# Query tiles 0 to 3 made in the gates' ring, and the attention's remaining projections spread over its units

## The chip, the cores and the metric

The kernel runs on one core of one Trainium2 chip. The core has a matrix engine (TensorE, PE in the profile; its weight loads are PEld), a vector engine (DVE), a scalar engine (ACT), GpSimd (POOL) and a queue engine (SyncE, SP) that here only issues DMAs. Every engine carries out its instructions in the order in which they stand; engines wait for each other on semaphores. The metric is the device time of one execution in microseconds, lower is better, as the median of the runs.

## The reference

One layer of a decoder trunk, in fp32, on 2048 tokens of width 1024:

```python
u = x * (1.0 + scale) + shift                       # from silu(c) @ w_ada + b_ada
q, k, v, a_gate, p_in, p_gate, m_a, m_p = split(u @ w_in)
a = sliding_window_sink_attention(q, k, v, sinks, bias, mask) * silu(a_gate)   # 16 heads of 64, 2 k/v heads, window 128
a = a @ w_attn_proj
p = group_linear(multiscale_causal_pool(p_in))      # windows 2, 4, 8, 16
p = (p * pool_scale) * silu(p_gate)
p = p @ w_pool_proj
y = ((sigmoid(m_a) * a + sigmoid(m_p) * p) @ w_out) * (1.0 + gate)
out = layer_norm(2 ** 0.25 * x + y)
```

## The kernel before

**Halves and stages.** The tokens are worked in two halves of 1024 (s = 0, 1), each in two parts of 512 columns (t = 0, 1). For each half there is a *ring* (functions `first_phase` and `second_phase`) and an *attention* (`attention`); then a stage that multiplies out both halves. In the trace the first ring lasts to about 417 us, the first attention to about 683, the second ring to 1018 and the second attention to about 1283.

**Products of three.** Each fp32 product is made of three matmuls on operands that are split in a high and a low part (`mm3`). The split of a weight is one ACT copy and one subtraction on DVE or POOL. A *k-step* is one block of 128 rows of the inner dimension: three matmuls of 128x512.

**The ring** makes two weight tiles of 128 outputs (a `Quad`, from here on a *pair*) for both parts of a half at once, by seven products of half size instead of eight: each product has 4 k-steps, 12 matmuls. So a pair takes 84 matmuls where four plain projections (two tiles by two parts, 8 k-steps each) take 96. Its weights need three splits of 1024 columns and one of 512, and four sums on POOL. A pair's four results come in PSUM banks or in SBUF (`p5`) and are handed to a `consume` function. Pairs are worked in groups of two; near the end there is a group with one pair, and a last group of two. A pair's weights lie in tiles W (two buffers) and A. Functions in `hooks` run other work at given ticks of the ring, counted from its start or, with a negative group number, in its last groups.

**What the ring makes.** The four gates for all tokens (16 pairs, results to DRAM in `gates_d`) and k with v (one pair). After its last group, `first_q` makes query tile 0 for both parts by plain projection, 48 matmuls.

**The attention** goes through 64 *units* n: head pair j = n // 8, part t, block b of 128 queries. In unit n, PE makes the scores of n (`lg<-kk,qs`), the transposes of unit n−2's weights (`pt<-ident,L`), a share of a projection, and the value products of n−2 (`pv<-pth,vv` and `pv<-ptl,vv`). ACT copies one half of the values of n−3 (`o<-pv`), scales rows, makes `pth`, and makes the exponentials (`L<-L,nm`). DVE makes the reciprocal (`sm`), adds the outputs (`o<-pv,o`), reduces the scores (`L<-lg,bt,nsink`), makes `ptl`, and scales rows. The projections are those of the pool input (`mix` tiles 0 to 7, whose weight lies split in DRAM) and of query tiles 1 to 7 (`q`, whose weight is loaded to W and split by one ACT copy and one POOL subtraction). Each tile is made for t = 0 and t = 1, a *slot* of 8 k-steps each. Before, the 30 slots fill units 0 to 59 with 4 k-steps in each unit; then the next stage's first products follow.

**What a finished slot sets off.** A query slot is *taken* (`take_q`: two ACT instructions and two DVE instructions `qs<-mm,qs`, which start when ACT's are done). A mix slot is copied by ACT (`vb<-mm` with two small copies), summed by POOL (`nxt`), reduced by DVE (`nxt<-nxt,mm`, the pool difference) and multiplied by POOL with its gate (`p<-nxt,pg`). The calls stand at the end of a unit, behind the unit's own work on each engine. Bias tiles (`bt<-e_rep`), gates and mix weights are loaded by SP.

Most instructions carry the line of a helper that keeps their program order (L56), so the profile is read by tile names. The functions, with the profile's line numbers:

Of the kernel before, what the change touches and what calls it, by code (L numbers as in the profile page):

```python
# [19 lines left out]
P = 128  # L20
# [39 lines left out]
def kernel(  # L60
# [60 lines left out]
    pin_d = [set_store(f"pin{s}") for s in range(2)]  # L121
    gates_d = {n: dp.tile([2, KT, 2, P, CH], F32, name=f"{n}_d") for n in ("ag", "pg", "ma", "mp")}
    y_d = dp.tile([S // P, P, KT, P], F32, name="y_d")

# [6 lines left out]
    def low(engine, dst, src, hi):  # L131
        engine.tensor_tensor(dst, src, as32(hi), ALU.subtract)  # L132
# [187 lines left out]
    def by_two(t):  # L320
        return t.rearrange("p (a c) -> p a c", a=2)
# [139 lines left out]
    def defer(ticks, f):  # L461
        due.append((now[0] + ticks, len(due), f))
# [269 lines left out]
    def moving_u():  # L732
        return (sets["B11"], sets["B21"]), (sets["T2"], sets["B22"])

    def first_q(ph, turn=None):

        raw, hi, lo = ph.spare(), ph.split(), ph.split()
        nc.sync.dma_start(raw, win[TQ])
        nc.scalar.copy(hi, raw)
        low(nc.vector, lo, raw, hi)  # L740
        accs = []
        for us in moving_u():
            acc, part = projection(us)
            part((hi, lo), 0, KT)
            if turn and not accs:
                turn(1)
            accs.append(acc)
        return accs

    def attention(ph, s, q0, nxt):  # L750
# [8 lines left out]

        def fetch(kind, m):  # L760
            hi, lo = ph.split(), ph.split()
# [107 lines left out]

        slots = []  # L870
        for j in range(KT):
            slots += [("mix", j, 0), ("mix", j, 1)]
            if j + 1 < KT:
                slots += [("q", j + 1, 0), ("q", j + 1, 1)]
# [8 lines left out]
        tiles = {0: fetch(*slots[0][:2])}  # L883
        parts, accs, sums = {}, {}, {}
# [36 lines left out]
        for n in range(N + 5):  # L921
            j, t, b = n // U, n // NB % 2, n % NB
            if n < N:
                lgs[n] = score_mms(j, n % U, b, qs[j, t])
# [71 lines left out]

            w = n // 4 + 1
            if n % 4 == 0 and 2 * w < len(slots):
                tiles[w] = fetch(*slots[2 * w][:2])
            if w in tiles and tiles[w][0] is not None:  # L1000
                raw, hi, lo = tiles[w]
                if n % 4 == 1:
                    act.copy(by_two(hi), raw)
                if n % 4 == 2:
                    low(pool, by_two(lo), raw, by_two(hi))
            if n % U == 2 and j + 1 < KT:
                bts[j + 1] = bias_tile(j + 1)
            for st in range(2):
                if n % U == 6 + 2 * st - (U if st else 0) and (m := j + 1 - st) < KT and ("q", m, st) in accs:
                    qs[m, st] = take_q(accs.pop(("q", m, st)))  # L1010
            for what in puts:
# [12 lines left out]
            for st in range(2):  # L1024
                if n % U == 3 + 2 * st and (j, st) in sums:
                    pgs[j, st] = ld("pg", gates_d["pg"][s, j, st])
                if n % U == ((4, 6 + (j + 1 < KT))[st]) and (j, st) in sums:
                    pl = pool_diff(j, sums.pop((j, st)), accs.pop(("mix", j, st)))
                    finish("p", pin_d[s], j, st, pl, pgs.pop((j, st)))
            for st in range(2):  # L1030
                if n % U == 2 + 2 * st and ("mix", j, st) in accs:
                    sums[j, st] = pool_sums(j, st, accs["mix", j, st])
            for x in [x for x in outs if n == x[0] * U + x[1] * NB + NB + 2]:
# [83 lines left out]
    def modulate(u, k):  # L1117
        dve.tensor_scalar(u, u, mod[:, 8 + k : 9 + k], mod[:, k : k + 1], ALU.mult, ALU.add)

    def gate_quads(s):  # L1120
        kv, turn = kv_quad(s)
        quads = [kv] if s else []
# [3 lines left out]
        last = quads[15:] if s else [kv, quads[15]]  # L1126
        return [quads[i : i + 2] for i in range(0, 14, 2)] + [quads[14:15], last], turn

# [14 lines left out]
    def head(ph):  # L1143
# [92 lines left out]

        groups, turn = gate_quads(0)
        grp = groups[0]
# [72 lines left out]
        ]  # L1311
        return groups, turn, opened, cb, rest

    def first_phase(ph, groups, turn, opened, cb, rest):
        hooks = {}
# [29 lines left out]
    def second_phase(ph, opened, groups, turn):  # L1345
        hooks = {(0, (8, 10)[i]): [lambda i=i: turn(i)] for i in range(2)}
# [29 lines left out]
        for half in range(2):  # L1376
            hooks.setdefault((-1, 3 + half), []).append(lambda half=half: fill_set("T2", half, u1_d["B12"]))
        return ring(ph, groups, opened, hooks, [], lambda tick: first_q(ph), True)

# [13 lines left out]
    def cols2(t, n):  # L1393
        return t[:, n * D : (n + 1) * D]
# [117 lines left out]
```

## Time and profile before

| | before |
|---|---|
| median of 3 runs | 1763.04 us (1761.94 to 1768.7) |
| the profiled execution | 1766.1 us, span 1763.9 us |
| mean clock of PE | 0.991 of full |
| PE, PEld | 97%, 81% of the span |
| DVE, ACT, POOL | 68%, 53%, 45% |
| DMA | 381.3 MB, 216 GB/s |

A row of the instructions in order of time has the start in us, the length in us, the engine, the line, the operation, output <- inputs by the program's names, the shape, how many instructions were merged into the row, and in brackets the idle time of the engine before it with what ended that. The length of a matmul is modelled and overlaps the next one's, so PE's pace is read from the starts.

### The profile page before, as it was taken

Reading aid. Unit: us, or ns where it says so; the run is one execution under the profiler, and the core shown is the slowest. Engines: PE = TensorE matmul, PEld = TensorE weight load, DVE = VectorE, ACT = ScalarE, POOL = GpSimd, SP = SyncE. Lnnn points to the kernel's source line nnn. Section 1 sums busy time; section 2 is a strip of 40 time slices with the busy share of each in tenths; the row PEclk is TensorE's granted clock in tenths of the full one; section 3 lists DMA queues with packets and bytes.
Section 4 is the critical chain, followed back from the end, with each engine's and each line's share of the span. In section 5 each row is a group of like instructions: output and inputs, shape, how many; then the busy total and the mean of one; then the engine's idle time right before and its main releaser. Section 6 shows DMA issues by size and latency. Waiting matters only on the chain. (4 is left out here: it accounts for less than half of the span.)

```text
span 1763.9 us, 24990 instructions
## 1 busy us (share of the span) xinstructions
PE 1702.4 (97%) x8248; PEld 1427.4 (81%) x8248; DVE 1206.9 (68%) x2178; ACT 934.1 (53%) x1973; POOL 794.2 (45%) x618
## 2 busy tenths in 40 slices
PE   6899999999999998999999999999999989999997
PEld 5688888878888887888788888888888867888785
DVE  5977665655777776766655367777867676764777
ACT  4644444545777775544444377777734343423452
POOL 2154444431356567534434125456763562364542
PEclk9999999999999999999999999999999999999998
DMA  9385767844354567787777634544796675789442
GB/s 364 117 289 174 269 208 270 273 145 132 108 174 147 171 217 288 249 288 253 258 264 261 232 96 135 177 159 141 265 349 215 197 256 169 240 302 386 162 143 108
DMA packets 180466, 381.30 MB, mean 216 GB/s; under 512 B 18785, under 2 KB 39281, under 8 KB 180337
## 3 DMA queue, kind: packets, MB, share of 16 engines
q1 hardware_dynamic: 173696, 363.92, 60.5%
q0 software_dynamic: 3552, 11.56, 1.7%
q10 hardware_dynamic: 3088, 4.23, 0.8%
q8 instruction: 65, 1.06, 0.3%
q14 instruction: 65, 0.52, 0.1%
HBM read 244.35 MB, written 138.44 MB: 217 GB/s over the span
## 5 line engine op out<-in xcount | busy, mean ns | idle before, releaser
L56 PE MATMUL mm<-set_B,w_set 128*128 128x512 f32 x3240 | 798.7, 395 | 14.5 <-ACT u L376 6.3
L56 PEld LDWEIGHTS mm<-set_B,w_set 128*128 128x128 f32 x3240 | 603.3, 189 | 142.6 <-DVE w_set L132 10.3
L56 PE MATMUL lg<-set_T,w_set 128*128 128x512 f32 x2088 | 509.1, 394 | 18.4 <-DVE w_set L132 11.0
L56 PEld LDWEIGHTS lg<-set_T,w_set 128*128 128x128 f32 x2088 | 391.4, 189 | 111.0 <-DVE w_set L132 17.9
L132 DVE TENSOR_TENSOR w_set<-W,w_set 128x1024 fp32r<-128x1024 f32 x162 | 227.9, 1407 | 185.8 <-ACT w_set L325 180.8
L325 ACT CAST w_set<-W 128x1024 fp32r<-128x1024 f32 x162 | 169.8, 1049 | 251.6 <-PE mm L56 190.3
L56 PE MATMUL mm<-set_T,w_set 128*128 128x512 f32 x1080 | 265.5, 394 | 0.0
L56 PEld LDWEIGHTS mm<-set_T,w_set 128*128 128x128 f32 x1080 | 200.5, 188 | 41.0
L294 POOL TENSOR_TENSOR W<-W,A 128x512 f32<-128x512 f32 x56 | 82.1, 1466 | 227.6 <-DMA W<-in_win_dram 63.6
L303 POOL TENSOR_TENSOR W<-W 128x512 f32<-128x512 f32 x56 | 80.5, 1438 | 174.5 <-DVE w_set L132 165.2
L56 DVE TENSOR_TENSOR o<-pv,o 64x128 f32<-64x128 f32 x256 | 72.3, 283 | 89.8 <-ACT o L56 86.9
L56 ACT ACTIVATE L<-L,nm 128x257 f32<-128x257 f32 (+1 forms) x256 | 127.1, 498 | 9.3 <-DVE nm L56 3.9
L298 POOL TENSOR_TENSOR W<-W 128x512 f32<-128x512 f32 x56 | 90.5, 1618 | 84.7 <-DVE w_set L132 75.6
L56 DVE CUSTOM_DVE_ANT_0 L<-lg,bt,nsink 128x256 f32<-128x256 f32 (+1 forms) x256 | 111.6, 473 | 5.0 <-PE lg L56 0.8
L299 POOL TENSOR_TENSOR W<-W 128x512 f32<-128x512 f32 x56 | 84.7, 1513 | 37.9 <-DMA W<-in_win_dram 21.9
L56 POOL TENSOR_TENSOR w_set<-W,w_set 128x1024 fp32r<-128x1024 f32 x14 | 33.7, 2404 | 139.6 <-ACT w_set L56 96.9
L56 POOL TENSOR_TENSOR p<-nxt,pg 128x512 f32<-128x512 f32 x32 | 41.7, 1302 | 105.5 <-DVE sm L56 101.8
L56 ACT COPY o<-pv 64x256 f32<-64x256 f32 x128 | 47.3, 370 | 78.0 <-PE pv L56 77.2
L56 DVE TENSOR_TENSOR ptl<-pt,pth 128x512 fp32r<-128x512 f32 (+1 forms) x128 | 85.7, 669 | 1.9 <-ACT pth L56 1.7
L56 PE MATMUL lg<-kk,qs 128*128 128x256 f32 (+1 forms) x512 | 80.5, 279 | 0.0
L56 ACT ACTIVATE L<-L,sm 128x256 f32<-128x256 f32 (+1 forms) x128 | 64.2, 502 | 29.8 <-DVE sm L56 29.8
L56 ACT CAST pth<-pt 128x512 fp32r<-128x512 f32 (+1 forms) x128 | 73.5, 574 | 10.3
(212 smaller groups left out, 2296.3 us busy)
## 6 DMA issues: line engine op xcount, KB each, us to landing
W<-in_win_dram SPq DMA_DIRECT2D x48, 512.0 KB, 5.5
w_set<-wmix_d SPq DMA_DIRECT2D x32, 512.0 KB, 5.4
W<-in_win_dram SPq DMA_DIRECT2D x34, 256.0 KB, 3.7
A<-in_win_dram SPq DMA_DIRECT2D x34, 256.0 KB, 5.1
ag_d<-sig SPq DMA_DIRECT2D x32, 256.0 KB, 3.8
pg_d<-sig SPq DMA_DIRECT2D x32, 256.0 KB, 4.0
ma_d<-sig SPq DMA_DIRECT2D x32, 256.0 KB, 4.0
mp_d<-sig SPq DMA_DIRECT2D x32, 256.0 KB, 4.0
```

Source lines behind the costliest of these rows:

```text
L56: return lambda *args, **kw: self.tc.keep_in_program_order(op(*args, **kw))
L132: engine.tensor_tensor(dst, src, as32(hi), ALU.subtract)
L294: e.tensor_tensor(self.w[:, 1, :], self.w[:, 2, :], self.a22, ALU.add)
L298: e.tensor_tensor(x[:, 1, :], x[:, 1, :], x[:, 0, :], ALU.subtract)
L299: e.tensor_tensor(x[:, 2, :], x[:, 0, :], x[:, 2, :], ALU.subtract)
L303: e.tensor_tensor(x[:, 3, :], x[:, 3, :], x[:, 1, :], ALU.subtract)
L325: a.copy(by_two(hi), raw)
```

## The change

Query tiles 0 to 3 are no longer projected by themselves. They are two more pairs (`q_quad`) at the end of the ring: tiles 2 and 3 in the group of one pair, tiles 0 and 1 in the last group (with k and v in the first half). Tile 0's two results stay in PSUM and are taken at the attention's start; the six results of tiles 1 to 3 go to DRAM (`q_d`) by SP and are loaded again (`raw_q`) two units ahead of their takes, at units 6, 8, 14, 16, 22 and 24. `first_q` is gone. The attention keeps the eight mix tiles and query tiles 4 to 7, 24 slots, in a written order. Their 192 k-steps are spread over units 0 to 59: 6 in unit 0, made ahead of its scores, 4 in units 5, 12, 19, 26, 32, 39, 46, 53 and 59, and 3 in the others. Query tiles are taken in the unit after their last k-step, pool sums are made in that unit too, and pool differences three or four units after the last k-step. The first mix tile is loaded into a W tile instead of two `w_set` tiles.

```diff
-    def first_q(ph, turn=None):
-        ...
+        order = (("mix", 0), ("mix", 1), ("mix", 2), ("mix", 3), ("mix", 4), ("q", 4), ("mix", 5), ("q", 5), ("q", 6), ("mix", 6), ("q", 7), ("mix", 7))
+        slots = [(kind, m, st) for kind, m in order for st in range(2)]
...
+        def upto(n):
+            return (0 if n == 0 else min(n + 1, 61)) * KT * len(slots) // 61
+
+        def unit_of(k):
+            return next(n for n in range(60) if upto(n + 1) > k)
+
+        first = [unit_of(KT * i) for i in range(len(slots))]
+        done = {x: unit_of(KT * i + KT - 1) for i, x in enumerate(slots)}
+
+        def project(n):
+            k = upto(n)
+            while k < upto(n + 1):
+                i = k // KT
+                end = min(KT * (i + 1), upto(n + 1))
+                if k == KT * i:
+                    accs[slots[i]], parts[i] = projection(us[slots[i][2]])
+                parts[i](tiles[i // 2][1:], k - KT * i, end - KT * i)
+                k = end
+
+        room = ph.weights().rearrange("p a c -> p (a c)").bitcast(F32R)
+        tiles = {0: fetch(*order[0], [cols2(room, n) for n in range(2)])}
...
         for n in range(N + 5):
             j, t, b = n // U, n // NB % 2, n % NB
+            if n == 0:
+                project(n)
             if n < N:
                 lgs[n] = score_mms(j, n % U, b, qs[j, t])
...
-            i = n // 2
-            if i < len(slots):
-                kind, m, st = slots[i]
-                if n % 2 == 0:
-                    accs[kind, m, st], parts[i] = projection(us[st])
-                parts[i](tiles[i // 2][1:], 4 * (n % 2), 4 * (n % 2) + 4)
+            if 0 < n < 60:
+                project(n)
...
+            for m in range(1, 4):
+                for st in range(2):
+                    at = 8 * m - 2 + 2 * st
+                    if n == at - 2:
+                        raw_q[m, st] = ld("raw_q", q_d[s][m, st])
+                    if n == at:
+                        qs[m, st] = take_q(raw_q.pop((m, st)))
+            for x in [x for x in done if x[0] == "q" and n == done[x] + 1]:
+                qs[x[1:]] = take_q(accs.pop(x))
...
+                if n == at + 3 + (st == 1 and m + 1 < KT):
+                    pl = pool_diff(m, sums.pop((m, st)), accs.pop(x))
+                    finish("p", pin_d[s], m, st, pl, pgs.pop((m, st)))
...
+    def q_quad(s, m, first):
+        def consume(ph, mi, t, src):
+            k = m + mi
+            if k == 0:
+                first[t] = src
+                return
+            x = src
+            if (mi, t) != (1, 1):
+                x = ph.c("qk")
+                nc.scalar.copy(x, src)
+            defer(2, lambda: sp.dma_start(q_d[s][k, t], x))
+        return Quad((win[TQ + m], win[TQ + m + 1]), consume)
...
+        quads += [q_quad(s, m, q0) for m in (2, 0)]
+        if s == 0:
+            quads.insert(-1, kv)
...
-        return ring(ph, groups, opened, hooks, [], lambda tick: first_q(ph, turn))
+        ring(ph, groups, opened, hooks, [], lambda tick: turn(1))
+        return q0
```

How this stands in the engines' streams is seen at three places. PE in the second attention, before, at units 30 and 31 (scores, transposes, projection, values):

```order
L56 MATMUL lg<-kk,qs 128x256 x4
L56 MATMUL pt<-ident,L 128x128 x4
L56 MATMUL mm<-set_T_235,w_set 128x512 x12
L56 MATMUL pv<-pth,vv 128x256
L56 MATMUL pv<-ptl,vv 128x256
L56 MATMUL pv<-pth,vv 128x256
L56 MATMUL pv<-ptl,vv 128x256
L56 MATMUL lg<-kk,qs 128x256 x4
L56 MATMUL pt<-ident,L 128x128 x4
L56 MATMUL mm<-set_B_576,w_set 128x512 x12
```
and the same two units after:

```order
L56 MATMUL lg<-kk,qs 128x256 x4
L56 MATMUL pt<-ident,L 128x128 x4
L56 MATMUL mm<-set_B_66,w_set 128x512 x9
L56 MATMUL pv<-pth,vv 128x256
L56 MATMUL pv<-ptl,vv 128x256
L56 MATMUL pv<-pth,vv 128x256
L56 MATMUL pv<-ptl,vv 128x256
L56 MATMUL lg<-kk,qs 128x256 x4
L56 MATMUL pt<-ident,L 128x128 x4
L56 MATMUL mm<-set_B_68,w_set 128x512 x9
```
Each unit's projection went from twelve matmuls to nine; all else in the unit stayed. DVE in the second attention, before, from `ptl` of unit 8 to `ptl` of unit 9, with the take of tile 1's second part (ISA is the reduction of the scores):

```order
L56 TENSOR_TENSOR ptl<-pt,pth 128x512
L56 TENSOR_SCALAR L<-L,sm 128x256
L56 SCALAR_TENSOR_TENSOR qs<-mm,qs 64x512 x2
L56 RECIPROCAL sm<-sm 128x2
L56 TENSOR_TENSOR o<-pv,o_10005 64x128 x2
```
and after:

```order
L56 TENSOR_TENSOR ptl<-pt,pth 128x512
L56 TENSOR_SCALAR L<-L,sm 128x256
L56 SCALAR_TENSOR_TENSOR qs<-raw_q,qs 64x512 x2
L56 SCALAR_TENSOR_TENSOR nxt<-nxt,mm 128x512
L56 RECIPROCAL sm<-sm 128x2
L56 TENSOR_TENSOR o<-pv,o_10218 64x128 x2
```
The take stands where it stood, reads the loaded tile in SBUF instead of a PSUM bank, and a pool difference now stands between it and the next unit's reciprocal. SP's queue at the end of the first ring, before, up to the first bias tiles:

```order
L56 DMA mp_d<-sig 128x512 x2
L764 DMA w_set<-wmix_d 128x1024
L765 DMA w_set<-wmix_d 128x1024
L56 DMA mp_d<-sig 128x512
L56 DMA bt<-e_rep 128x2x256 x2
```
and after:

```order
L56 DMA q_d<-p_3368 128x512
L750 DMA w_set<-wmix_d 128x1024
L751 DMA w_set<-wmix_d 128x1024
L750 DMA w_set<-wmix_d 128x1024
L751 DMA w_set<-wmix_d 128x1024
L56 DMA q_d<-qk 128x512
L56 DMA bt<-e_rep 128x2x256 x2
L743 DMA pg<-pg_d 128x512
L743 DMA ag<-ag_d 128x512
L743 DMA raw_q<-q_d 128x512
```
The bias tiles now stand behind the weights of two mix tiles and behind the last query store; the first raw query tile is loaded behind a gate of each kind.

More of the change, by code (lines that the diff above doesn't have):

```diff
@@ L122 @@
     gates_d = {n: dp.tile([2, KT, 2, P, CH], F32, name=f"{n}_d") for n in ("ag", "pg", "ma", "mp")}
+    q_d = [dp.tile([4, 2, P, CH], F32, name=f"q{s}_d") for s in range(2)]
     y_d = dp.tile([S // P, P, KT, P], F32, name="y_d")
@@ L733, in moving_u @@
         return (sets["B11"], sets["B21"]), (sets["T2"], sets["B22"])
-    def first_q(ph, turn=None):
[L737 to L748, printed above, removed]
     def attention(ph, s, q0, nxt):
@@ L1125, in gate_quads @@
                 quads.append(gate_quad(s, name, base, m, kind))
-        last = quads[15:] if s else [kv, quads[15]]
-        return [quads[i : i + 2] for i in range(0, 14, 2)] + [quads[14:15], last], turn
+        quads += [q_quad(s, m, q0) for m in (2, 0)]
+        if s == 0:
+            quads.insert(-1, kv)
+        n = len(quads) - 3
+        return [quads[i : i + 2] for i in range(0, n, 2)] + [quads[n : n + 1], quads[n + 1 :]], turn, q0
     def gate_modulation(ph, m, cb):
@@ L1235, in rest_sums @@
             minus(xs[4 + i][0], xs[4 + i][0], ts[i])
-        groups, turn = gate_quads(0)
+        groups, turn, q0 = gate_quads(0)
         grp = groups[0]
@@ L1311, in head, with first_phase @@
         ]
-        return groups, turn, opened, cb, rest
-    def first_phase(ph, groups, turn, opened, cb, rest):
+        return groups, turn, q0, opened, cb, rest
+    def first_phase(ph, groups, turn, q0, opened, cb, rest):
         hooks = {}
@@ L1342, in first_phase, with second_phase @@
             at(-1, 3 + half, lambda half=half: build(ph, "T2", half, b12_d))
[L1343 to L1345 removed]
+        ring(ph, groups, opened, hooks, [], lambda tick: turn(1))
+        return q0
+    def second_phase(ph, opened, groups, turn, q0):
         hooks = {(0, (8, 10)[i]): [lambda i=i: turn(i)] for i in range(2)}
@@ L1377, in second_phase @@
             hooks.setdefault((-1, 3 + half), []).append(lambda half=half: fill_set("T2", half, u1_d["B12"]))
-        return ring(ph, groups, opened, hooks, [], lambda tick: first_q(ph), True)
+        ring(ph, groups, opened, hooks, [], None, True)
+        return q0
     def pairs(make):
```

52 lines of the change are left out of this document (23 added, 29 removed).

## The prediction

> **What bounds the kernel now.** I read the page first, then busy time by stage, then instructions in order of time at a ring's end and inside the attention.
>
> ```profile
> span 1763.9 us, 24990 instructions
> PE 1702.4 (97%) x8248; PEld 1427.4 (81%) x8248; DVE 1206.9 (68%) x2178; ACT 934.1 (53%) x1973; POOL 794.2 (45%) x618
> ```
> ```profile
> 690.00:1010.00 320.00, 311.40 (x1365) 256.19 (x1366) 194.08 (x210) 148.88 (x229) 119.36 (x84) 0.99 0.75 261
> 1020.00:1280.00 260.00, 260.00 (x1497) 228.09 (x1496) 194.78 (x609) 198.50 (x589) 140.11 (x109) 1.00 0.51 164
> ```
> The columns are stage, length, then busy time of PE, PEld, DVE, ACT, POOL, PE's clock, DMA share, GB/s. In the second half's ring (upper row) and attention (lower row) PE does not rest, at full clock. DVE is busy 75% of the attention and ACT 76%, so an average says that both could go a quarter faster. Busy PE is modelled, so the true price of a matmul comes from the starts of long rows (start, length, instruction):
>
> ```profile
> 1001.73 5.60 PE L56 MATMUL lg<-set_T,w_set 128*128 128x512 f32 x24
> 1007.17 5.60 PE L56 MATMUL mm<-set_B,w_set 128*128 128x512 f32 x24
> 1012.61 2.88 PE L56 MATMUL mm<-set_T,w_set 128*128 128x512 f32 x12
> 1015.33 2.88 PE L56 MATMUL mm<-set_B,w_set 128*128 128x512 f32 x12
> 1018.05 0.64 PE L56 MATMUL lg<-kk,qs 128*128 128x256 f32 x4
> ```
> From 1001.73 to 1007.17 are 24 matmuls: 0.2267 us each. From 1007.17 to 1018.05 is `first_q`, 48 matmuls, 10.88 us; the attention's first score follows at once.
>
> The attention is the place to look at closely. Unit 30 of the second attention, where a query tile is taken, and the unit on each side:
>
> ```profile
> 1135.62 0.57 ACT L56 COPY vb<-mm 128x512 f32<-128x512 f32 x1
> 1135.69 0.68 DVE L56 SCALAR_TENSOR_TENSOR nxt<-nxt,mm 128x512 f32<-128x512 f32 x1
> 1136.29 0.16 DVE L56 RECIPROCAL sm<-sm 128x2 f32<-128x2 f32 x1
> 1136.32 0.17 ACT L56 COPY carry<-mm 128x16 f32<-128x16 f32 x1
> 1137.15 0.37 ACT L56 COPY o<-pv 64x256 f32<-64x256 f32 x1 [0.66 <-PE pv L56]
> 1138.98 0.69 DVE L56 TENSOR_TENSOR ptl<-pt,pth 128x512 fp32r<-128x512 f32 x1
> 1139.68 0.19 ACT L56 ACTIVATION_READ_ACCUMULATOR L<-L,nm 128x1 f32 x1
> 1140.63 0.28 PE L56 MATMUL pv<-pth,vv 128*128 128x256 f32 x1
> 1141.13 0.63 PE L56 MATMUL lg<-kk,qs 128*128 128x256 f32 x4
> 1141.95 3.02 PE L56 MATMUL mm<-set_T,w_set 128*128 128x512 f32 x12
> 1143.95 1.19 ACT L56 ACTIVATE qs<-mm 64x512 fp32r<-64x512 f32 x2
> 1144.81 0.28 PE L56 MATMUL pv<-pth,vv 128*128 128x256 f32 x1
> 1145.16 1.39 DVE L56 SCALAR_TENSOR_TENSOR qs<-mm,qs 64x512 fp32r<-64x512 f32 x2 [1.06 <-ACT qs L56]
> 1145.30 0.63 PE L56 MATMUL lg<-kk,qs 128*128 128x256 f32 x4
> 1146.57 0.17 DVE L56 RECIPROCAL sm<-sm 128x2 f32<-128x2 f32 x1
> 1146.76 0.58 DVE L56 TENSOR_TENSOR o<-pv,o 64x128 f32<-64x128 f32 x2
> 1148.19 0.69 DVE L56 TENSOR_TENSOR ptl<-pt,pth 128x512 fp32r<-128x512 f32 x1
> 1148.96 0.28 PE L56 MATMUL pv<-pth,vv 128*128 128x256 f32 x1
> ```
> A unit is 4.17 us (scores at 1141.13 and 1145.30): 12 projection matmuls, 2.72, and 1.45 of scores, transposes and values. Its value matmuls need ptl. In a plain unit ptl ends at 1139.67 and the value starts at 1140.63: 0.96 to spare. But the take at the end of unit 30 runs as a chain, ACT's exponentials, ACT's qs (1.19), DVE's qs (1.39), then the next unit's reciprocal, additions, reductions and ptl, which ends at 1148.88. The value starts at 1148.96: 0.08 to spare. The twelve matmuls just cover a take.
>
> **The change part by part.** *PE's count.* Per half, a ring gains two pairs of 84 matmuls (seven products of 12) and loses `first_q`'s 48: +120, +27.2 us. The attention's projections fall from 720 to 576: −144, −32.6 us. Together −24 per half, −48 × 0.2267 = −10.9 us, if PE stays the limit. The ring's added splits, sums and copies lie beside PE: there DVE works 194 of 320 us, ACT 149, POOL 119. That cover is PE's 19 us per pair; nothing there depends on `first_q`.
>
> *The attention's pace.* Sixty units now hold 3 k-steps, 9 matmuls, in most units, and 4 in units 5, 12, 19, 26, 32, 39, 46, 53 and 59 (6 in unit 0). A plain unit of 9 lasts 4.17 − 0.68 = 3.49 us, with 0.96 − 0.68 = 0.28 to spare, so it still holds. A take does not. Its chain is bound to its own unit's score: ptl ends 1148.88 − 1141.13 = 7.75 us after it, however few matmuls PE has, since pt follows the score directly. The value came after 7.83; two shortened units bring it forward by 1.36. PE then waits 1.36 − 0.08 = 1.28; with one unit of four k-steps 0.60. PE is in order, and the next score stands behind that value, so the wait is lost. The fourteen takes per half are at units 6, 8, 14, 16, 22, 24 (from DRAM) and 27, 30, 38, 40, 43, 45, 53, 55; of these 38, 45 and 53 touch a long unit. 11 × 1.28 + 3 × 0.60 = 15.9, for both halves +31.8 us. Bounds: zero if the chain shrank with the unit, 36 if no long unit helped.
>
> *What now stands behind a take.* Pool differences fall into the units of the takes at 8, 14, 24, 38 and 53, on DVE behind qs and ahead of the reciprocal: 0.60 each (1135.69 to 1136.29), 3.0 per half, +6.0 us. Elsewhere a difference falls into DVE's idle time. ACT idles 0.77 in a 3.49 us unit (3.49 less the 2.72 from 1137.15 to 1139.87); vb with its two small copies is 0.87 and is absorbed. The weight's copy is 1.03:
>
> ```profile
> 1157.40 1.03 ACT L56 CAST w_set<-W 128x1024 fp32r<-128x1024 f32 x1
> ```
> It now meets a take at unit 30 (+1.03, ahead of qs), vb at 20 and 35 (0.87 + 1.03 − 0.77 − 0.28, some 0.8 each) and follows a take at 46 (0.2): 2.8 per half, +5.6 us. Three such copies fewer per half free nothing: while PE is the limit, ACT's rest is worth nothing. Bounds: 0, where DVE's lateness already covers ACT's, and 8.
>
> *Six takes per half read SBUF, not PSUM.* The trace of before has no such instruction. The nearest rows are the present one and a subtraction of the same length from two SBUF operands (shortest, median, longest ns):
>
> ```profile
> L56 DVE SCALAR_TENSOR_TENSOR qs<-mm,qs x64: 683/688/694, 414.2 to 1254.2; 64x512 fp32r<-64x512 f32 x64
> L56 DVE TENSOR_TENSOR k_lo<-spare,k_hi x61: 677/693/1800, 88.1 to 976.8; 128x512 fp32r<-128x512 f32 x61
> ```
> ```profile
> L56 DVE TENSOR_TENSOR k_lo<-spare,k_hi 128x512 fp32r<-128x512 f32 x61 | 60.1, 990 | 26.6 <-ACT k_hi L56 14.4 <-DMA ain_T_split<-k_hi 3.1 <-DMA ag_d<-sig 2.0
> ```
> ```profile
> 1142.39 1.31 POOL L56 TENSOR_TENSOR a<-o,ag 128x512 f32<-128x512 f32 x1 [2.53 <-DVE o L56]
> ```
> From PSUM it never lengthens; from SBUF it takes 0.99 on average, and a POOL operation is some 1.3. I take the mean difference, 0.30, for each of 12 per half: 3.6, +7.2 us. Ends: 0 (both have one floor, and no projection waits for a bank that could come free earlier), and 1.1 each, 26 us.
> The Trainium skill, "SBUF — State Buffer", section "SBUF: two separate sides", states why: a VectorE operation with two SBUF inputs and a GpSimd operation that reads SBUF lock one port pair in turn, and the loser "fully blocks". By that rule this edit speaks against the change; with POOL busy 140 of 260 us and 1.31 per operation, an estimate is 0.54 × 0.65 = 0.35 per instruction, 8.4 us, against 0 if PSUM's price held; both rows above agree with the rule.
>
> *The start.* `first_q` covered the first take and the first bias tile for 10.9 us. Now 18 matmuls, 4.1 us, stand before the first score, and the bias tile's issue stands behind four weight loads and the last query store, which wait for the ring's end.
>
> ```profile
> bt<-e_rep SPq DMA_DIRECT2D x2, 256.0 KB, 4.9
> ```
> ```profile
> 420.60 0.35 DVE L56 CUSTOM_DVE_ANT_0 L<-lg,bt,nsink 128x128 f32<-128x128 f32 x1
> 422.85 0.28 DVE L56 TENSOR_SCALAR L<-L,sm 128x128 f32<-128x128 f32 x1
> ```
> Issued about 1 us after the ring's last matmul, it lands 4.9 later; from the first reduction to scaled rows were 2.5 us (420.60 to 423.13): 8.4. PE reaches the first transposes after 27 matmuls, 6.1, and three groups of score size, 1.4: 7.5. I take 1.0 per half, +2.0 us (ends 0 and 8).
>
> *DMA.* Seven stores and six loads of 256 KB per half against a DMA share of 0.51 to 0.75: nothing, unless a load is late (below).
>
> Sum: −10.9 + 31.8 + 6.0 + 5.6 + 7.2 + 2.0 = +41.7 us. The profiled execution took 1766.1 us around its span of 1763.9, 3.1 above the median of 1763.04; so 1808 against itself, **1805** as a median.
>
> **Rivals.** *The waits are hidden: faster.* If DVE and ACT catch up before the values, only −10.9 is left: 1752. For it speaks 75% busy time: 195 us of DVE work fits into the new 218 us attention. Against it speaks the 0.08: a take's chain is latency, not load. It decides where the mean wait per take is under 10.9 / 28 = 0.39 us.
>
> *Half of it.* If a chain loses with one shortened unit only, 28 × 0.60 = 16.8, less 10.9, and the other terms fall into the same slack: 1769, no change that can be told (0.5%, some 9 us, is the bound).
>
> *Later loads as well.* A raw query tile is issued two units, some 7 us, ahead of its take, on SP's queue among loads and stores that wait for POOL. POOL is late at places already, and such loads are slow:
>
> ```profile
> 633.87 0.69 DVE L56 SCALAR_TENSOR_TENSOR nxt<-nxt,mm 128x512 f32<-128x512 f32 x1 [1.49 <-POOL nxt L56]
> pg<-pg_d SPq DMA_DIRECT2D x2, 256.0 KB, 5.2
> ```
> With 1.5 us for each of 12 loads, 18 more: 1823. Against it: most such loads are issued early, when a buffer comes free.
>
> **How the numbers follow.** Takes that stall PE, as summed: 0.74. Late loads on top: 0.11. Half: 0.08. Hidden: 0.07. The range goes from takes alone with a fifth of their wait absorbed (1763 − 10.9 + 25 = 1777, say 1775) to the late loads (1822). Slower by over 0.5%: 0.85; within it 0.08; faster 0.07.
>
> **What would show it.** Right: scores 3.49 us apart in plain units, about 4.8 in the unit after a take; PE idle before values there, released by DVE's ptl; rings 27 us longer, attentions some 6 us shorter instead of 33 (32.6 less the waits' 26.3 per half); qs from raw_q longer than 0.69 at times. Wrong: units of 3.5 us after takes too, or ptl ending earlier after its take's score than 7.7 us.

## The result, and the profile after

The changed kernel takes 1814.7 us (median of 4 runs, 1812.78 to 1817.31) against 1762.49 in the runs beside it: ratio 1.0298, 95% interval 1.0278 to 1.0319, slower. The forecast was 1805 (1775 to 1822). The profiled execution took 1815.8 us around its span of 1814.0. From its page, the span and the share of PE:

```profile
span 1814.0 us, 25046 instructions
PE 1718.8 (95%) x8200; PEld 1426.4 (79%) x8200; DVE 1232.6 (68%) x2200; ACT 951.7 (52%) x1997; POOL 804.7 (44%) x628
```

PE has 48 matmuls fewer, as counted, and is busy for 95% instead of 97% of a longer span. The stages can be cut at the starts of the first and the last score (`lg<-kk,qs`) of each half, so that `first_q` falls into the ring:

| us | first ring | first attention | second ring | second attention | rest |
|---|---|---|---|---|---|
| before | 417.7 | 257.3 | 343.0 | 260.6 | 485.3 |
| after | 454.9 | 249.4 | 371.5 | 254.8 | 483.4 |
| difference | +37.2 | −7.9 | +28.5 | −5.8 | −1.9 |
| forecast | +31.3 | −10.4 | +31.3 | −10.4 | 0 |

The forecast is put by the same cut. The 18 matmuls that unit 0 makes ahead of its scores stand before the first score and so fall into the ring:

```profile
1071.68 4.24 PE L56 MATMUL mm<-set_B,W 128*128 128x512 f32 x18
1075.76 1.11 PE L56 MATMUL lg<-kk,qs 128*128 128x256 f32 x8
```

A ring so gains 120 + 18 matmuls, 31.3 us, and an attention loses 144 + 18, 36.7, against the 26.3 us of waits of the forecast, start included. By this table the attentions lost 2.5 and 4.6 us more than forecast, the first ring is 5.9 longer and the second 2.8 shorter. Busy time by stage, second half, ring and attention (columns as before):

```profile
720.00:1070.00 350.00, 344.64 (x1513) 284.85 (x1514) 202.97 (x217) 158.01 (x243) 128.30 (x92) 0.99 0.70 245
1080.00:1330.00 250.00, 231.86 (x1309) 195.97 (x1310) 200.74 (x597) 193.14 (x576) 132.44 (x104) 0.99 0.47 161
```

In the attention PE is no longer busy throughout: 231.86 of 250 us, and its clock is 0.99 instead of 1.00. DVE and ACT are at 80% and 77% and are waited for. The waits of PE in that stretch (what waited, for whom, us in total, times, longest); before there were none in the second attention:

```profile
PE pv L56 <- ACT pth L56: 9.5, 11, 2.8
PE pv L56 <- DVE ptl L56: 7.5, 16, 0.8
```

A plain unit and the unit after a take, in order of time (units 27 and 28 of the second attention, query tile 4's first take):

```profile
1187.61 0.63 PE L56 MATMUL lg<-kk,qs 128*128 128x256 f32 x4
...
1190.48 1.18 ACT L56 ACTIVATE qs<-mm 64x512 fp32r<-64x512 f32 x2
...
1191.07 0.63 PE L56 MATMUL lg<-kk,qs 128*128 128x256 f32 x4
...
1191.69 1.39 DVE L56 SCALAR_TENSOR_TENSOR qs<-mm,qs 64x512 fp32r<-64x512 f32 x2 [1.04 <-ACT qs L56]
...
1194.72 0.69 DVE L56 TENSOR_TENSOR ptl<-pt,pth 128x512 fp32r<-128x512 f32 x1
...
1195.46 0.38 PE L56 MATMUL pv<-ptl,vv 128*128 128x256 f32 x1 [0.55 <-DVE ptl L56]
...
1195.93 0.64 PE L56 MATMUL lg<-kk,qs 128*128 128x256 f32 x4
```

Scores 3.46 us apart, then 4.86: ACT's qs, DVE waiting 1.04 for it, DVE's qs, then ptl, which ends 7.80 us after the take's score (1187.61 to 1195.41), and the value waits for it. That is the chain of the prediction, with its 7.75 and its 4.8.

What it did not have is seen shortly before, around unit 25, where a query tile from DRAM is taken beside POOL's operations on the stage tiles:

```profile
1172.65 4.35 POOL L56 TENSOR_TENSOR p<-p,p 128x512 f32<-128x512 f32 x3
...
1174.13 3.42 DVE L56 SCALAR_TENSOR_TENSOR qs<-raw_q,qs 64x512 fp32r<-64x512 f32 x2
...
1177.58 0.69 DVE L56 SCALAR_TENSOR_TENSOR nxt<-nxt,mm 128x512 f32<-128x512 f32 x1
...
1178.44 0.51 ACT L56 ACTIVATE L<-L,sm 128x256 f32<-128x256 f32 x1 [3.66 <-DVE sm L56]
...
1179.61 0.58 PE L56 MATMUL pv<-pth,vv 128*128 128x256 f32 x1 [2.83 <-ACT pth L56]
```
```profile
1176.00:1180.00 4.00, 1.17 (x5) 0.59 (x3) 3.92 (x10) 1.50 (x4) 1.01 (x1) 0.90 0.89 283
1180.00:1184.00 4.00, 3.78 (x15) 3.40 (x15) 2.47 (x10) 3.11 (x12) 1.02 (x1) 0.50 1.05 410
```

DVE's two instructions need 3.42 instead of 1.39 while POOL's three run, a pool difference stands behind them, ACT waits 3.66 for the reciprocal, PE 2.83 for ACT. Then, in the second row of the windows, PE runs at half its clock (0.50). So this unit and the next took 7.77 and 6.39 us. All instructions of the takes, by tile (count, shortest, median, longest ns), and the landing of the loads of raw_q:

```profile
L56 DVE SCALAR_TENSOR_TENSOR qs<-mm,qs x40: 683/690/694, 452.7 to 1303.4; 64x512 fp32r<-64x512 f32 x40
...
L56 DVE SCALAR_TENSOR_TENSOR qs<-raw_q,qs x24: 685/933/1727, 477.0 to 1175.9; 64x512 fp32r<-64x512 f32 x24
```
```profile
DMA to landing us min/median/max: 2.5/2.8/3.4
```

From PSUM nothing lengthens; from SBUF twelve stay at 0.69 and the other twelve take 1.18 to 1.73. The loads land in at most 3.4 us of the 7 that they have.

And the first ring. Two DMAs are issued 2 us apart, the gate's column (1040 packets, written element by element) and the last pair's weights; POOL waits for those weights, and PE for what hangs on POOL's sums:

```profile
373.31 0.40 ACTq L1385 DMA_DIRECT2D gate_d<-mod  x1
```
```profile
375.55 1.15 SPq L289 DMA_DIRECT2D A<-in_win_dram  x2
```
```profile
388.73 1.29 POOL L295 TENSOR_TENSOR W<-W,A 128x512 f32<-128x512 f32 x1 [16.71 <-DMA A<-in_win_dram]
```
```profile
394.71 2.50 PE L56 MATMUL lg<-set_T,w_set 128*128 128x512 f32 x5 [4.07 <-ACT lg L369]
```
```profile
380.00:388.00 8.00, 8.00 (x37) 6.53 (x36) 1.23 (x1) 1.74 (x3) 0.00 (x0) 1.00 1.02 78
...
396.00:400.00 4.00, 4.00 (x10) 3.04 (x10) 1.22 (x1) 1.53 (x2) 0.29 (x1) 0.50 0.06 22
```

The DMA engines are fully busy (1.02) and move 78 GB/s. PE loses 4.07 us and then some 3.4 more at half clock (6.8 us of it): 7.5 us, which covers the 5.9 that the first ring has over its forecast (elsewhere in this ring PE waits some 2 us less than before).

### The profile page after: what moved, and what is told of

It is laid out like the page before. It is cut to its first block, busy times and chain, and to the rows that moved or that the text cites. A ratio compares the mean times of both kernels' runs of the same rounds, so it can differ in the third digit from the quotient of the medians.

```text
span 1814.0 us, 25046 instructions
## 1 busy us (share of the span) xinstructions
PE 1718.8 (95%) x8200; PEld 1426.4 (79%) x8200; DVE 1232.6 (68%) x2200; ACT 951.7 (52%) x1997; POOL 804.7 (44%) x628
## 5 line engine op out<-in xcount | busy, mean ns | idle before, releaser
L56 PE MATMUL mm<-set_B,w_set 128*128 128x512 f32 x3024 | 757.2, 397 | 11.8 <-DVE w_set L133 7.0
L56 PEld LDWEIGHTS mm<-set_B,w_set 128*128 128x128 f32 x3024 | 567.3, 190 | 131.8 <-DVE w_set L133 9.6
L56 PE MATMUL lg<-set_T,w_set 128*128 128x512 f32 x2232 | 542.6, 394 | 18.6 <-DVE w_set L133 10.3
L56 PEld LDWEIGHTS lg<-set_T,w_set 128*128 128x128 f32 x2232 | 419.6, 189 | 114.7 <-DVE w_set L133 14.9
L56 PE MATMUL mm<-set_T,w_set 128*128 128x512 f32 x1008 | 252.7, 395 | 0.0
L304 POOL TENSOR_TENSOR W<-W 128x512 f32<-128x512 f32 x60 | 84.3, 1406 | 187.9 <-DVE w_set L133 177.8
L299 POOL TENSOR_TENSOR W<-W 128x512 f32<-128x512 f32 x60 | 95.9, 1599 | 97.3 <-DVE w_set L133 88.2
L300 POOL TENSOR_TENSOR W<-W 128x512 f32<-128x512 f32 x60 | 94.8, 1579 | 45.7 <-DMA W<-in_win_dram 31.1
L56 POOL TENSOR_TENSOR nxt<-vb 128x512 f32<-128x512 f32 (+3 forms) x32 | 35.1, 1097 | 158.7 <-ACT vb L56 85.6
L56 PE MATMUL pv<-ptl,vv 128*128 128x256 f32 x248 | 71.0, 305 | 16.9 <-DVE ptl L56 16.5
L56 PE MATMUL pv<-pth,vv 128*128 128x256 f32 x248 | 70.6, 297 | 16.4 <-ACT pth L56 16.0
L56 DVE TENSOR_TENSOR k_lo<-spare,k_hi 128x512 fp32r<-128x512 f32 x61 | 61.7, 1016 | 29.3 <-ACT k_hi L56 8.1
```

The lines of the kernel that those rows point to most:

```text
L56: return lambda *args, **kw: self.tc.keep_in_program_order(op(*args, **kw))
L299: e.tensor_tensor(x[:, 1, :], x[:, 1, :], x[:, 0, :], ALU.subtract)
L300: e.tensor_tensor(x[:, 2, :], x[:, 0, :], x[:, 2, :], ALU.subtract)
L304: e.tensor_tensor(x[:, 3, :], x[:, 3, :], x[:, 1, :], ALU.subtract)
```

## The experiments

My theory: each take is a chain through ACT and DVE that outlasts a unit of 3 k-steps. The rivals in them: a take's work costs the same wherever it stands; POOL and the queues are late by themselves. "Unit n" below is from score n to score n + 1. The kernel before, run beside each version, came to 1762.5 to 1767.4 us, so a difference between two versions is known to some 5 us.

**The count alone (e1).** The kernel before, with three of the four k-steps in each unit; the fourth is left out, and with it a quarter of the projections.

```diff
-                parts[i](tiles[i // 2][1:], 4 * (n % 2), 4 * (n % 2) + 4)
+                parts[i](tiles[i // 2][1:], 5 * (n % 2), 5 * (n % 2) + 3)
```

> The kernel before, with 3 of the 4 k-steps in each of the attention's units 0 to 59 (k-steps 3 and 4 of every slot are left out, 9 matmuls instead of 12 a unit); nothing else moves. PE has 2 x 60 x 3 x 0.2267 = 81.6 us less. Latency theory (a take's chain ends 7.75 us after its unit's score however few matmuls there are): every one of the 28 takes costs 1.28 us, the weight's copies a little, some 40 us come back: 1762 - 82 + 40 = 1721 (1713 to 1730), plain units 3.49 us and the unit after a take 4.8. Rival, the waits are hidden since DVE and ACT are busy only 75%: 1681, all units 3.5 us. Rival, the loss of the changed kernel is in its ring and its loads: also 1681, since here neither has changed.

1742.54 us, ratio 0.9865 (0.9834 to 0.9896). The attentions fall by 15.2 and 17.1 us, not by the 40.8 of their matmuls. Waits of PE in the second one:

```profile
PE pv L56 <- DVE ptl L56: 8.0, 15, 0.6
PE pv L56 <- ACT pth L56: 3.7, 14, 0.4
```

Plain units are 3.47, units after a take 4.79 (two in eight), with nothing else changed: 1.31 per take. The chain theory holds for the takes. The total was above the 1721 expected: the waits of the attentions come to 49 us instead of 40, and in the profile the last stage is 11 us longer than before. PE waits 20 us there instead of 12 and runs 13.7 us at half clock instead of 6.8; why stays open.

**The takes in pieces (e2).** Each take is split by heads over two units.

```diff
-                    at = 8 * m - 2 + 2 * st
+                    at = 8 * m - 3 + 2 * st
...
-                        qs[m, st] = take_q(raw_q.pop((m, st)))
+                        qs[m, st] = take_q(raw_q[m, st], None, (0,))
+                    if n == at + 1:
+                        take_q(raw_q.pop((m, st)), qs[m, st], (1,))
```

> The changed kernel, with each take spread over two units: the half for one head (one ACT and one DVE instruction) at the end of one unit, the other at the end of the next; the takes start one unit earlier, so that none is later. The same instructions, the same work. Latency theory: half a take is 0.62 on ACT, inside ACT's idle 0.77, and 0.69 on DVE; the chain is late by 0.3 and a plain unit has 0.28 to spare, so the takes' 32 us and the 6 of the differences behind them go, some raw takes still wait for POOL: 1778 (1770 to 1788). Rival, load: DVE and ACT have the same work to do and the attention stays as long: 1812 to 1817.

1807.65 us, ratio 1.0226 (1.0191 to 1.026): a miss, 7 us gained of the 37 expected. Half a take still stands ahead of its unit's ptl on DVE, behind ACT, and costs 0.25 to 0.6 twice; units 15, 22 and 25 still take 5.3 to 5.9.

**Split in the ring (e3).** Tiles 1 to 3 are scaled and split in the ring, stored as both parts, and loaded into qs. Their takes are gone.

```diff
-                x = ph.c("qk")
-                nc.scalar.copy(x, src)
-            defer(2, lambda: sp.dma_start(q_d[s][k, t], x))
+            ...
+            defer(2, lambda: [sp.dma_start(q_d[s][k, t, :, h, :], as32(x[h])) for h in range(2)])
...
-                        qs[m, st] = take_q(raw_q.pop((m, st)))
+                        sp.dma_start(as32(qs[m, st]), q_d[s][m, st])
```

> The changed kernel, with tiles 1 to 3 scaled and split in the ring, straight from its PSUM banks or SBUF, stored as both parts (512 KB instead of 256 each) and loaded into qs: the attention has 8 takes per half instead of 14, and none reads SBUF. Latency theory with the port: the waits in units 7 to 9, 15 to 17 and 23 to 26 of the changed kernel go, 11 us in the first and 15 in the second half: 1789 (1783 to 1795); the ring stays as long, since its ACT and DVE have room. Rival, load: DVE loses 12 x 1.4 and ACT 12 x 1.2 us of work in the attentions, so at most 17 us: 1798. Rival, ring: the work moved there lengthens it, 1815 or more.

1816.74 us, ratio 1.0282 (1.0255 to 1.031): a miss. That is the number of the ring rival, but not its place: the rings are only 1.6 and 1.8 us longer than in the changed kernel. The units behind those takes did fall to 3.47, but in the second attention units 18, 19, 29 and 30 rose to 5.2 to 7.7, and units 1 and 2 to 7.4 and 6.5. The longest new wait of POOL in the second attention:

```profile
POOL p L56 <- DMA pin_T<-p: 19.1, 2, 10.9
```

It writes a stage tile whose store must have landed. In the new order the pool differences of an odd tile's part 1 and of the next tile's part 0 come one unit apart (before: five), and the second write waits for the stores that the first sets off.

**POOL's subtractions (e4).** The four subtractions in `finish` are left out; their stores go out unsubtracted.

```diff
-            pool.tensor_tensor(t1, x, t1, ALU.subtract)
...
-            pool.tensor_tensor(b21, b21, t1, ALU.subtract)
...
-            pool.tensor_tensor(b11, t1, b11, ALU.subtract)
```

> The changed kernel without the four subtractions on POOL in finish that form T1, T2, T4 and T3 of the attention's outputs (the stores write the operands instead): POOL has some 21 us less to do per attention, in bursts of three. Port theory (a DVE instruction with two SBUF operands waits until POOL's has ended): the DVE instructions qs from raw_q fall from 0.93 us at the median towards 0.69, units 15 and 25, 6.3 to 7.8 us now, lose 1 to 3 us each, the half clock behind them goes: 1803 (1797 to 1809). Rival, the raw tiles' loads or the takes alone make these units long: 1812 to 1817.

1807.16 us, ratio 1.0228 (1.0199 to 1.0256), as expected. DVE's groups (count, busy us, mean ns):

```profile
L56 DVE SCALAR_TENSOR_TENSOR qs<-raw_q,qs 64x512 fp32r<-64x512 f32 x24 | 18.0, 750 | 6.9 <-ACT qs L56 6.5
```

In the changed kernel this row reads 26.0 us, mean 1082; now 22 of the 24 take 0.69. Unit 25 falls from 6.4 and 7.8 to about 5, unit 15 from 6.7 and 6.3 to 4.7, which is the plain price of a take; the rest was POOL's work beside a raw take.

**The low part later (e5).** DVE's two instructions of a take stand a unit later.

```diff
+                    if n == at + 1:
+                        take_low(raw_q.pop((m, st)), qs[m, st])
```

> The changed kernel, but the two DVE instructions of a take stand one unit after its two ACT instructions, behind that unit's ptl and scaled rows, so DVE no longer waits for ACT there. The chain theory: ACT's 1.19 us meets 0.76 us of idle time (0.43 late), and DVE's 1.39 (1.8 from raw tiles) falls into the 1.62 us in which DVE waits for ACT's copy of o. The unit after a take falls from 4.8 to about 3.9 us; 14 takes per half x 0.9 x 2 = 25 us: 1790 us (1783 to 1798). Rival, load: a take's work has to be done in some unit and costs the same wherever it stands: 1812 to 1817, with the 1.3 us only moved one unit on.

1816.32 us, ratio 1.0291 (1.0266 to 1.0316): a miss. For projected tiles it helped (units 43 to 47 of the second attention lose 1.3 us together instead of 2.5); for raw tiles the loss moved one unit on, and units 18, 23 and 24 came to 5.8 to 6.7 us.

**Three steps (e6).** ACT's first instruction, a unit later its second, a unit later both of DVE.

```diff
+                if n == at:
+                    qs[x[1:]] = take_q(accs[x], None, (0,) if late else (0, 1))
+                if n == at + 1 and late:
+                    take_q(accs[x], qs[x[1:]], (1,))
+                if n == at + 1 + late:
+                    take_low(accs.pop(x), qs[x[1:]])
```

> The changed kernel, but each take is spread over three units: ACT's first instruction, ACT's second one unit later, and both DVE instructions one unit after that (query tile 5's first part in two units, since it is needed sooner). The chain theory: 0.6 us fits into ACT's 0.76 idle, 1.39 into DVE's 1.62, so units after takes go to 3.5 to 3.7 us; what stays is POOL's hold on DVE's SBUF reads and the pool differences. 14 x 1.2 x 2 = 34 us less: 1781 us (1773 to 1792). Rival, load: no less than 1805, as the takes spread over two units without this order gave (1807.7).

1806.36 us, ratio 1.0238 (1.0212 to 1.0263): a miss in the total, not at the takes. DVE at the end of unit 7:

```profile
1098.60 1.41 DVE L56 SCALAR_TENSOR_TENSOR qs<-raw_q,qs 64x512 fp32r<-64x512 f32 x2
1100.04 0.17 DVE L56 RECIPROCAL sm<-sm 128x2 f32<-128x2 f32 x1
1100.26 0.58 DVE L56 TENSOR_TENSOR o<-pv,o 64x128 f32<-64x128 f32 x2
```

DVE waits for nobody, and tile 4's take leaves units 28 and 29 at 3.47 and 3.59. But at unit 18, with POOL late (it had waited 6.20 us for a gate tile):

```profile
1137.03 2.86 DVE L56 SCALAR_TENSOR_TENSOR qs<-raw_q,qs 64x512 fp32r<-64x512 f32 x2
...
1137.93 0.59 ACT L56 COPY vb<-mm 128x512 f32<-128x512 f32 x1 [1.09 <-POOL nxt L56]
```

So units 18, 23, 24 and 30 of the second attention keep 1.6 to 2.7 us each over their price.

**The gate's column (e7).** Its DMA is issued in the last group of the first ring.

```diff
-            nc.scalar.dma_start(gate_d.rearrange("k p -> p k"), mod[:, 16:24], allow_slow_non_contiguous=True)
...
+        at(-1, 1, lambda: act.dma_start(gate_d.rearrange("k p -> p k"), mod[:, 16:24], allow_slow_non_contiguous=True))
```

> The changed kernel, but the DMA that writes the gate's column element by element (1040 packets, 14.8 us to landing, issued at 373.3 in the changed kernel) is issued in the last group of the first ring, behind the weight loads. Theory: it holds the DMA engines (share 1.02 at 78 GB/s from 380 to 388) while the last pair's weights (A) load, 13.0 us to landing; PE then waits 4.1 us and runs 6.8 us at half clock. Without it the first ring is 7 us shorter: 1808 us (1805 to 1811). Rival: the load is late for the gates' stores ahead of it on SP's queue: no difference, 1813 to 1817, and PE's wait of 4 to 6 us in the last group stays.

PE at the place of its 4.07 us wait:

```profile
391.68 2.88 PE L56 MATMUL lg<-set_T,w_set 128*128 128x512 f32 x12
394.40 2.88 PE L56 MATMUL mm<-set_B,w_set 128*128 128x512 f32 x12
```

The wait and the half clock are gone, the weights land in 3.6 us, and the first score comes at 448.8 us instead of 454.9. In the four kernels with this edit (e7, e9, e11, e12) it comes at 447.4 to 448.8, in the other eight on the new ring at 454.2 to 459.2: for the ring the theory is shown, and what is left of the ring's growth, 31.1 us, is its matmuls. In the total the 6 us are not seen: 1816.25, ratio 1.0294 (1.0264 to 1.0324). Its profiled span is 2.3 us shorter than the changed kernel's, with 2.3 us more in the second ring and 1.2 in the second attention; why the median does not show the gain stays open.

**Two together (e8), and the queues (e9).** e8 is e3 with the three steps of e6 for the projected tiles. In e9 POOL's own queue also takes the stores, and the gate tile, the first bias tile and the column are moved.

```diff
-                put(pool if n >= 64 else sp, *what)
+                put(pool, *what)
...
-                if n == at + 2:
+                if n == at + 1:
                     pgs[m, st] = ld("pg", gates_d["pg"][s, m, st])
```

> Two earlier edits together: tiles 1 to 3 are scaled and split in the ring and loaded as both parts, and the eight takes of projected tiles are spread over three units. Chain theory: no take and no DVE instruction on raw_q is left on a critical place in the attention; against the run with three steps alone (1806.4) the raw takes' rest goes (units 16, 18, 23, 24 of the second half: 0.57, 1.76, 2.68, 2.14 over their price), some 8 per half: 1790 us (1782 to 1800). Rival, queue: what is left is POOL's and SP's lateness (POOL waited 8.2 us for a store of a stage tile when the tiles were split in the ring), which this edit brings back: 1803 to 1812.

> As the run before it in this call, and the queues eased: the stores of gated products stand on POOL's own queue instead of SP's, the gate tile of the pool branch is loaded one unit earlier, the first bias tile is loaded through ACT's queue ahead of the first takes, and the gate's column is written behind the ring's weight loads. Queue theory: POOL is late because its loads and stores stand on SP behind waiting ones; units 17 to 31 come to 3.5 to 4.3 us, the start loses 1 to 2 us less per half and the first ring 7: 1775 us (1768 to 1788). Chain theory alone: POOL's lateness does not reach PE once the raw takes are gone, so only the ring's 7 and the start's 3 go: 10 less than the run before it. Rival: POOL's issues cost its own time (0.73 us for each of 32 stores per half) and hold DVE longer: no gain against the run before it.

1808.73 (ratio 1.0227, 1.0202 to 1.0253) and 1812.26 us (1.025, 1.0219 to 1.028): the queue rival came true, and easing the queues did not help in the total. By stage, e9 has 7.5 us less than e8 in the first ring (the column), the same attentions within 1 us, and a last stage that is 9 us longer, for which I have no cause. Its first bias tile is no longer late: units 1 and 2 of the second attention take 2.6 and 5.3 us, in e8 7.4 and 7.4. Now no take is left to hide POOL's wait, and in e9 it stands free at unit 18, on POOL, ACT and PE:

```profile
1123.29 1.65 POOL L56 DMA_DIRECT2D pin_T<-p  x3
1130.61 1.29 POOL L56 TENSOR_TENSOR p<-nxt,pg 128x512 f32<-128x512 f32 x1 [5.67 <-DVE ptl L56]
```
```profile
1135.31 0.58 ACT L56 COPY vb<-mm 128x512 f32<-128x512 f32 x1 [4.66 <-POOL nxt L56]
```
```profile
1137.66 0.38 PE L56 MATMUL pv<-pth,vv 128*128 128x256 f32 x1 [3.30 <-ACT pth L56]
```

POOL issues three stores and then waits 5.67 us before it writes p again (the named releaser had long been done; the stores landed 6.0 us after their issue). So its sums are late, ACT's copy of the next slot waits 4.66 for their input buffer, and PE for ACT.

**The differences apart (e10, e11, e12).** Three or four units lie between POOL's operations and the next write of the stage tile. e10 has this alone, e11 with the three steps and the column, e12 with e8's split in the ring, the column, and the first bias tile on ACT's queue.

```diff
-                if n == at + 3 + (st == 1 and m + 1 < KT):
+                apart = {(2, 0): 2, (4, 0): 1}.get((m, st), 0)
+                if n == at + 3 + apart:
```

> The changed kernel, with only the pool differences moved: every second difference (odd tile, part 1) one unit earlier, that of tile 2 part 0 two units later and that of tile 4 part 0 one unit later, with their gate loads, so that three or four units lie between POOL's four operations on the stage tiles and the next write of the first of them (one unit in the changed kernel). Stage-tile theory: POOL waits some 6 us there (6.2 before 1138.8, 6.0 before 1183.0) for the store, then catches up and holds DVE's qs; units 15 to 17 and 25 to 26 lose 2 to 4 us each over the takes' 1.3. Apart, they fall to about 4.8: 6 per half and the half-clock periods in the attentions (6.8 us each half, 3.4 lost) go: 1798 us (1792 to 1804). Rival: POOL is late for its own work, DVE's long qs come from any POOL operation: 1809 to 1817.

> The run before it, with each take in three steps as in e6 and the gate's column written later as in e7. If takes, stage tile and column are the three causes and add up: 1806.4 less 6 to 8 per half at units 18, 23, 24 and 30, less 6 in the first ring: 1786 us (1779 to 1795). If POOL's lateness has another cause: 1798 to 1806, with units 18 and 23 to 24 still over 5 us.

> Takes of projected tiles in three steps, tiles 1 to 3 split in the ring and loaded as both parts, the first bias tile through ACT's queue, the column later, and the pool differences apart. In e9 the attentions lost 6.9 and 5.8 us at units 18 and 19 and 8.2 and 8.0 at 29 and 30 (first and second half), all behind POOL's wait for the store of a stage tile. If that is the cause: 1812.3 less 26 to 29: 1785 us (1777 to 1792), units 18 and 29 at 3.5 to 4.2. If not: those two units keep over 5 us each, 1800 to 1812. Even the lower end stays above the 1764 of before, since the rings' 27 us per half leave 11 us to be gained at most, and W's copies, vb and the start still cost some 8 per half.

e10: 1817.94 us (1.0309, 1.0291 to 1.0328), a miss: units 15, 17 and 25 fell to 4.9 to 5.3 as expected, but unit 28 rose to 8.5 and 7.3. e11: 1809.58 (1.0253, 1.0227 to 1.028), a miss, for the same reason. SP's longest wait there, and POOL behind it:

```profile
SPq L743 <- DVE qs L56: 8.2, 1, 8.2
```
```profile
1161.52 1.30 POOL L56 TENSOR_TENSOR p<-nxt,pg 128x512 f32<-128x512 f32 x1 [11.38 <-DMA pg<-pg_d]
```

The gate tiles share three buffers (`ld`) with the raw query tiles. A load waits on SP until DVE has done with one, POOL waits 11.38 us for the gate, and units 26 and 28 take 8 to 9 us.

In e12 raw tiles use no such buffer, no DVE and no ACT: 1776.75 us (1773.01 to 1780.43), ratio 1.0071 (1.0045 to 1.0096), just under the 1777 to 1792 expected. From its page, its busy time from 1060 to 1290, and the longest waits of PE there:

```profile
span 1771.3 us, 25061 instructions
```
```profile
1060.00:1290.00 230.00, 225.18 (x1316) 194.56 (x1315) 188.47 (x582) 184.83 (x562) 131.85 (x105) 1.00 0.54 182
```
```profile
PE pv L56 <- DVE ptl L56: 2.4, 6, 0.6
PE pt L56 <- DVE L L56: 1.1, 2, 0.8
```

The attentions are 231.6 and 236.2 us, against 220.6 and 223.9 by matmuls alone (the table's 257.3 and 260.6 less 36.7), so 11.0 and 12.3 us of waits are left. The clock stays at 1.00. Units 18 and 29 are plain; the scores of units 28 to 30:

```profile
1154.88 0.64 PE L56 MATMUL lg<-kk,qs 128*128 128x256 f32 x4
...
1158.35 0.63 PE L56 MATMUL lg<-kk,qs 128*128 128x256 f32 x4
...
1161.82 0.63 PE L56 MATMUL lg<-kk,qs 128*128 128x256 f32 x4
```

With the same matmuls, 38 us of the 52 lost are back. Against e8, units 18, 19, 29 and 30 give some 12 and 9 us (first and second attention), where the spacing acts; the first four units give some 2 and 6, where the bias tile acts, and the first ring 9, mostly the column's. No version that makes the whole result beats the kernel before: in e12 the rings stay longer by 29.7 and 31.3 us, the attentions are shorter by 25.7 and 24.4, and the last stage by 3.5, since no half clock fell into it (6.8 us before); no edit aimed at that.

## Why the prediction was right, point by point

*PE's count.* 8248 to 8200 matmuls, as worked out. The second ring's +28.5 for 31.3 us of matmuls fits their price, since PE waits 6.1 us in it instead of 9.1; the prediction's "PE does not rest" was not right for that ring, whose row has 311.40 of 320 us. In the first ring the step that failed is "DMA: nothing, unless a load is late", with lateness looked for in the attention only: the longer ring put a weight load 2 us behind the gate's column, and e7 shows 6 us for it, which is the whole of the ring's 5.9. (The seven stores of that step are six.)

*The attention's pace.* Plain units 3.47 (forecast 3.49), units after a take 4.77 to 4.85 (4.8), with one long unit 4.80 for unit 46, 0.63 lost (0.60). e1 shows the same price without the rest of the change. "However few matmuls PE has" is what it came to; "hidden" and "half of it" fall with e1 already. (By matmuls the new attention is 221 to 224 us from first to last score, not 218.)

*What stands behind a take.* Pool differences: in the second attention units 39 and 54 lose 1.12 and 1.11 (forecast 1.20 each with a long unit), unit 9 1.48 (1.88). ACT's weight copies: unit 31 loses 2.29 (1.28 + 1.03), units 21 and 36 0.77 and 0.81 (0.8). Right to some tenths.

*Reading SBUF.* This is the term of the attention that was mis-sized: 0.39 per instruction on the mean (1.082 less 0.690), not 0.30, and not spread evenly. It gathers where a raw take stands beside three POOL operations in a row (3.42 for 1.39), delays ACT and PE for 2.8 us, and costs PE its clock. e4, which leaves only POOL's subtractions out, gains 7.5 us against the changed kernel (known to some 5), of the size of the whole term of 7.2; it takes work from POOL too, so not all of it need be the reads. The rule of the Trainium skill that the prediction named ("SBUF — State Buffer", "SBUF: two separate sides") agrees with both rows; its estimate of 0.35 was nearer than mine.

*The start.* Units 1 to 3 lose 1.6 us in the first attention and 2.1 in the second, against the same units before less their matmuls (forecast 1.0 each).

*Later loads.* The raw tiles land in 2.5 to 3.4 us and no take waits for them. That rival fell; loads were late elsewhere (the weights in the ring, gate tiles in e6 and e11).

*The sum.* The waits of the two attentions came to 28.8 and 30.9 us (249.4 and 254.8 less 220.6 and 223.9), forecast 26.3. At units 15, 17, 25 and 26 the losses were larger than their terms, at units 7, 9, 39 and 54 smaller; that the sum fits so closely is in part chance. The profiled span grew by 50.1 us, 8.4 more than the 41.7 forecast: the first ring has 5.9 of them and the attentions 7.1, while the second ring gives back 2.8 and the last stage 1.9.

What the prediction did not see is why the waits are hard to remove. I expected the takes to be one cause; there are three, and they stand in line. Alone, the three steps gave 8 us, the split in the ring −2, the spacing −3 (each known to some 5 us); the three together, with the column and the first bias tile moved, gave 38. Whether the split and the spacing would do without the three steps is not shown: no run has those two alone.

## What to carry to other kernels

Where engines work in order and hand over every few microseconds, read the spare time at the hand-over, not the share of busy time: 0.08 us to spare gave the price of a take to 0.1 us, while 75% busy time suggested that there was room. And when an experiment takes a cause away and the time stays, look at the rows of the place itself before the theory is dropped: here the takes fell to plain pace while the next late engine, POOL behind a store or a shared buffer, took over the wait. Moving writes of a single-buffered tile from five units apart to one makes a store's landing time part of the critical path.

## What the runs showed of the hardware

Waits of PE of only 1.2 to 2.8 us were followed by a halved clock. In the attentions of the changed kernel it stood at 0.50 from 513.6, 581.8 and 1179.2 us on, for 3.4, 3.4 and 6.8 us (some 6.8 lost in all). In the 3.4 us before each of these, the longest wait was 1.89 us, 1.21 us and the first 2.4 us of the wait of 2.83, and PE was busy for 1.1, 1.7 and 1.0 us. The attentions of before and of e12 have no such period. The Trainium skill ("TensorE: Matmul & The Clock Gate", "What's actually happening") puts the fall after "≥1 idle window (~3.4µs)"; the trace agrees with the length of a period (3.4 or 6.8 us) but shows it after windows in which PE had still worked for 1.0 to 1.7 us. And one DMA of 4 KB in 1040 packets kept the DMA engines busy (share 1.02 at 78 GB/s) for some 8 us, and a load of 256 KB issued 2 us behind it took 13.1 us instead of 3.6.
